# One matmul for the high and low part of the activations, in a two-block fp32 transformer kernel

## The chip, the cores and the metric

The kernel runs on one core of a Trainium2 chip, in one launch. The metric is the device time in microseconds (us). On the core five engines with queues of their own run at once: TensorE (PE, matmuls, with its weight loads as PEld), VectorE (DVE), ScalarE (ACT), GpSimd (POOL) and SyncE (SP, which here issues the DMAs). They wait for each other through semaphores.

## The reference

Everything is fp32, 256 tokens of width 1024. The first block has two layers, the second one; `@` is an fp32 product. Cut to what matters:

```
# first block, each of 2 layers
z = rms_norm(x, norm1_g) @ w_in          # latents, q/k/v of GLA, S5 input, 3 x 1024 gates
merged = sum over b of sigmoid(gate_b) * (mixer_b(z) @ w_br_b)     # MLA, GLA, S5
x = x + merged @ w_out
x = x + square(relu(rms_norm(x, norm2_g) @ w_ff1)) @ w_ff2         # 1024 -> 4096 -> 1024
# second block, 1 layer
z = rms_norm(x, g_pre_mix) @ w_in                     # q, k, v of 24 heads, GLU input, 2 gates
u = (a + b) * sigmoid(g + b)                          # GLU, 1024 channels
c = silu(layer_norm(depthwise_conv_31_taps(u) + b_dw)) @ w_conv_out + b_conv_out
merged = sigmoid(z_ga) * (dilated_attention(q, k, v) @ w_attn_out) + sigmoid(z_gc) * c
x = x + rms_norm(merged @ w_mix_out)
g, up = split(rms_norm(x) @ w_ffn_in)                 # 2 x 2816
x = x + rms_norm((silu(g) * up) @ w_ffn_out)
```

## The kernel before, in words

**Split operands.** TensorE multiplies fp32r, which keeps fewer bits than fp32. So every operand is taken apart into a high part H (ACT `Copy` into an fp32r tile, L160; L163 with a scale) and a low part L = x - H (DVE, L161; L164 with a scale). A product is H·H + H·L + L·H, three matmuls into one PSUM accumulator.

**The weight stream.** The weights come in units of 128x1024 (a row of eight 128x128 blocks). SP starts the DMA of a unit into `raw` (three buffers), ACT makes `wH` and DVE `wL` (four buffers for both together); a unit is fetched three units ahead of the one in use (`AHEAD = 3`).

**Feature-major units.** `f_unit` (L967) is the commonest use of a unit: 128 output features for 256 tokens. `mm_f` (L166) walks eight steps of the contraction, and in each step puts the 256 tokens through three times:

```
nc.tensor.matmul(ps, H[:, w], aH[:, i, :], start=(i == 0), stop=False)             # L169: weights H, activations H
nc.tensor.matmul(ps, H[:, w], aL[:, i, :], start=False, stop=False)                # L170: weights H, activations L
nc.tensor.matmul(ps, L[:, w], aH[:, i, :], start=False, stop=(i == nk - 1))        # L171: weights L, activations H
```

The result takes half of a PSUM bank: the tile `mm` has 128x512, of which `ps[:, :S]` (S = 256) is written. There are two `mm` tiles. One operation then takes it out (`evac`): an ACT copy, tanh, relu or square, or a DVE multiply. The activations lie in two tiles `hH` and `hL`, [128, 8, 256] each. There are 240 such units: the projections w_in of both blocks (38 in each layer of the first block, 56 in the second), w_ff1 (32 in each layer) and both halves of w_ffn_in (44). `mm_f`, or the same three matmuls written out, also serve the eight units of the conformer's output (`conv_out`, eight steps), the eight tiles of the S5 GLU (`s5_glu_tile`, four steps), the branch projections and the attention output.

**Token-major units.** `mm_t` (L173 to L177) puts 512 weight columns past 128 tokens into the accumulator `acc` (five buffers); w_ff2, w_ffn_out, w_out, w_mix_out and the v projections use it. In the FFN stages the units alternate: one `f_unit` (24 matmuls of 256 columns) and one token-major unit (12 matmuls of 512 columns).

**The order of the work.** The order of units and side work (the mixers' steps, the convolution) is written out by hand as strings of tokens; a scheduler then places each instruction on its engine's queue by priorities (taking a result out of PSUM has a raised one). In each engine the instructions run in the resulting order.

**The convolution of the second block.** `conv_gen` takes 31 taps for eight channel tiles `u`, two tiles at a time: DVE starts a sum (L1282), adds a tap times `u` (L1285, 128x256 each), and adds products that ACT made (L1278, 128x512). Its inputs `u` come out of 16 f-units (`g2th`, `ga`, L1451). `chan_sum` then adds the eight sums (L1305 to L1307) and sums over channels on TensorE (L1310); the layer norm and `conv_out` follow. Beside this run the q and k units of the attention and its scores (L1382, L1383).

Of the kernel before, what the change touches and what calls it, by code (L numbers as in the profile page):

```python
# [17 lines left out]
P = 128  # L18
# [17 lines left out]
# columns of the packed per-partition parameters of one layer of the first block  # L36
# [50 lines left out]
class Plan:  # L87
    """Program order: weight units (with what uses them) and side work."""
# [62 lines left out]
def make(k, tc, ins, out, dbg=None):  # L151
    """Fills k with the helpers; returns the plan."""
# [13 lines left out]
    def mm_f(ps, H, L, aH, aL, nk, off=0, m=P):  # L166
        for i in range(nk):
# [3 lines left out]
            nc.tensor.matmul(ps, L[:, w], aH[:, i, :], start=False, stop=(i == nk - 1))  # L171

# [41 lines left out]
    k.__dict__.update(split=split, mm_f=mm_f, mm_t=mm_t, sm=sm, rsq=rsq, mm_tile=mm_tile,  # L214
# [42 lines left out]
def pair_of(h):  # L257
    return lambda c: (h[0], h[1], c)
# [6 lines left out]
def residual_raw(k, t, accs, scale, g, dst):  # L265
    """x[:, t] += accs (times scale); x times g into dst, transposed."""
# [18 lines left out]
def norm_full(k, t, rsn, ss, gb, dst):  # L285
    """rsn[:, t] = rsqrt(mean(x^2) + eps); the normed x into dst, transposed; gb holds g in every row."""
# [8 lines left out]

def row_tile(k, i, name):
# [5 lines left out]
def post_residual(k, t, accs, gb, eps=EPS * D):  # L302
    """x[:, t] += accs rsqrt(sum(accs^2) + eps) gb; gb holds sqrt(D) g."""
# [40 lines left out]
def new_h(k):  # L344
    hH = k.act.tile([P, 8, S], F32R, tag="hH", name="hH")
    hL = k.act.tile([P, 8, S], F32R, tag="hL", name="hL")
    return hH, hL


# ---------------------------------------------------------------- S5  # L350
def s5_setup(k, l, st):
    """First part of what doesn't depend on the activations. The sequence is cut into 64 chunks of 4 steps:
    inside a chunk the output is a short convolution (k.W), chunk inputs go to the states by st.ET, states to
    the outputs by st.F, and the states at the chunk ends are scanned in a rotating frame (tables st.C, st.Sn,
    decay st.D). Parameters lie as [2 groups x 64 states, pair of groups, re/im, 16]; "s" has re and im
    exchanged."""
# [81 lines left out]
def s5_powers(k, st, name, nk, x, xs, ct, op):  # L438
    """[128, 8, nk, 16]: x times powers of lambda, for the four pairs of a channel tile, re and im."""
# [14 lines left out]
def s5_expand(k, dst, src):  # L454
    """Each half of the states to its own 16 of the 32 channels; the rest of dst stays zero."""
# [5 lines left out]
def s5_tile_prep(k, st, ct):  # L461
    """Matrices of one channel tile."""
# [30 lines left out]
def s5_tables(k, st):  # L493
    """Rotating frame of the scan over the chunks."""
# [101 lines left out]
def s5_run(k, l, st, prep):  # L596
    """prep: make what doesn't depend on the activations on the way."""
# [12 lines left out]
def s5_gelu(k, l, st):  # L610
    """2 * gelu(y), and gelu(y) split."""
# [16 lines left out]
def s5_glu_tile(k, l, st, n, H, L, off):  # L628
    nc = k.nc
    ps = k.mm_tile()  # L630
    k.mm_f(ps[:, :S], H, L, st.gH, st.gL, 4, off)
    th = k.t1("gluth")
    nc.scalar.activation(th, ps[:, :S], AF.Tanh, scale=0.5, bias=st.hb[:, n:n + 1])
# [5 lines left out]
# ---------------------------------------------------------------- GLA  # L639
def gla(k, l, st):  # L640
    """Needs st.gq (scaled), st.gk, st.kg, st.gv, st.sr (2 silu(r)); leaves st.goH, st.goL."""
# [24 lines left out]
    nc.vector.tensor_mul(qt, st.gq, E1)  # L666
# [189 lines left out]
def mla_attn(k, l, st, hf):  # L856
    """Heads 4 hf .. 4 hf + 3; needs st.qn, st.kn (per token tile), st.v; writes st.moH, st.moL."""
# [1084 lines left out]
```

## Time and profile before

| | |
|---|---|
| runs | 1485.37, 1485.79, 1486.06 us; median 1485.79 |
| span of the profiled execution | 1482.4 us |
| PE busy | 1440.2 us, 97% of the span, 10580 matmuls |
| PEld (weight loads, beside PE) | 1299.2 us, 88% |
| DVE busy | 1019.1 us, 69% |
| ACT busy | 840.1 us, 57% |
| DMA | 243.13 MB in, mean 164 GB/s |

The profiled execution's own time is its span, first instruction to last; the runs' times are 3 to 4 us above it. A row of the timeline gives an instruction's start and duration. Matmuls are pipelined, so their durations overlap, and what one of them costs is the distance from one start to the next. A granted clock (PEclk) of 1.00 is TensorE's 2.4 GHz, its upper level.

### The profile page before, as it was taken

The numbers are of one execution on the slowest core, as the hardware profiler recorded it, in microseconds if no ns is written. First come the engines' busy times: TensorE is split into PE (matmuls) and PEld (weight loads), VectorE is DVE, ScalarE is ACT, GpSimd is POOL, SyncE is SP. The second block draws the span as 40 slices with busy tenths as digits, with TensorE's granted clock in tenths as the row PEclk, the third lists the DMA queues.
The fourth block names the chain that finished last, engine by engine and source line by source line (L and its number), as shares of the span: only waits on it lengthen the run. The fifth ranks groups of instructions, "written<-read, shape, count | busy, mean of one in ns | idle before, by whom it ended". The sixth has DMA issues, their size and how long they took to land.

```text
span 1482.4 us, 26521 instructions
## 1 busy us (share of the span) xinstructions
PE 1440.2 (97%) x10580; PEld 1299.2 (88%) x10580; DVE 1019.1 (69%) x1876; ACT 840.1 (57%) x1469; POOL 48.6 (3%) x51
## 2 busy tenths in 40 slices
PE   8999999989999999989999999999999999899998
PEld 6979899778889899788988999989888989799997
DVE  7976777687455668566566555579988856765555
ACT  6855567465744556355546444465576574644443
POOL 1000100000000000012000000000000000000000
PEclk9999999999999999999999999999999999999999
DMA  6622344555455653235446555575544545355553
GB/s 223 207 86 97 108 162 152 163 171 183 160 165 186 209 165 94 81 130 171 155 164 218 189 185 186 188 234 178 179 146 121 167 143 206 126 195 185 185 185 114
DMA packets 71060, 243.13 MB, mean 164 GB/s; under 512 B 7864, under 2 KB 11656, under 8 KB 70936
## 3 DMA queue, kind: packets, MB, share of 16 engines
q1 hardware_dynamic: 70936, 241.43, 49.9%
q8 instruction: 83, 1.36, 0.4%
q14 instruction: 41, 0.34, 0.1%
HBM read 237.17 MB, written 4.23 MB: 163 GB/s over the span
## 4 chain that ended last, share of the span: by engine, by line
PE 72%; DVE 9%; ACT 3%; issue 2%; POOL 2%; DMA 1%; POOLq 0%; DVEq 0%; ACTq 0%; SPq 0%
PE mm L169 13%; PE mm L170 13%; PE mm L171 13%; PE acc L175 7%; PE acc L176 7%; PE acc L177 7%; DVE wL L161 3%; POOL rsq L184 2%; ACT wH L160 2%; DVE cv L1285 1%; PE acc L1409 1%; DMA raw<-in_wst_dram 1%; PE tr L1404 1%; PE acc L1382 1%; PE acc L548 1%
## 5 line engine op out<-in xcount | busy, mean ns | idle before, releaser
L161 DVE TENSOR_TENSOR wL<-raw,wH 128x1024 fp32r<-128x1024 f32 (+1 forms) x410 | 495.9, 1211 | 253.7 <-ACT wH L160 250.7
L160 ACT ACTIVATE wH<-raw 128x1024 fp32r<-128x1024 f32 (+1 forms) x410 | 429.2, 1047 | 379.7 <-PE mm L170 199.1
L169 PE MATMUL mm<-hH,wH 128*128 128x256 f32 x1920 | 553.5, 289 | 7.0 <-ACT gt L1038 3.5
L170 PE MATMUL mm<-hL,wH 128*128 128x256 f32 x1920 | 548.5, 286 | 3.2 <-DVE hL L164 3.2
L171 PE MATMUL mm<-hH,wL 128*128 128x256 f32 x1920 | 547.9, 286 | 0.0
L169 PEld LDWEIGHTS mm<-hH,wH 128*128 128x128 f32 x1920 | 368.5, 192 | 21.0 <-ACT hH L163 5.3
L170 PEld LDWEIGHTS mm<-hL,wH 128*128 128x128 f32 x1920 | 368.9, 192 | 8.8 <-DVE hL L164 4.4
L171 PEld LDWEIGHTS mm<-hH,wL 128*128 128x128 f32 x1920 | 368.9, 192 | 2.4 <-issue 1.9
L175 PE MATMUL acc<-wH,fH 128*128 128x512 f32 x344 | 135.3, 393 | 0.0
L176 PE MATMUL acc<-wL,fH 128*128 128x512 f32 x344 | 134.9, 392 | 0.0
L177 PE MATMUL acc<-wH,fL 128*128 128x512 f32 x344 | 134.1, 390 | 0.0
L1285 DVE SCALAR_TENSOR_TENSOR cv<-u,ppt,cv 128x256 f32<-128x256 f32 x184 | 78.6, 478 | 0.4
L177 PEld LDWEIGHTS acc<-wH,fL 128*128 128x128 f32 x344 | 64.6, 188 | 14.1
L175 PEld LDWEIGHTS acc<-wH,fH 128*128 128x128 f32 x344 | 64.9, 189 | 11.2
L176 PEld LDWEIGHTS acc<-wL,fH 128*128 128x128 f32 x344 | 64.9, 189 | 10.3
L160 ACT ACTIVATE fH<-ffr 128x256 fp32r<-128x256 f32 x64 | 26.6, 416 | 67.6 <-DVE ffr L1191 67.5
L161 DVE TENSOR_TENSOR fL<-ffr,fH 128x256 fp32r<-128x256 f32 x64 | 27.1, 424 | 23.2 <-ACT fH L160 23.2
L175 PE MATMUL acc<-wH,mH 128*128 128x512 f32 x96 | 37.9, 395 | 0.3 <-ACT mH L163 0.3
L176 PE MATMUL acc<-wL,mH 128*128 128x512 f32 x96 | 37.8, 394 | 0.0
L177 PE MATMUL acc<-wH,mL 128*128 128x512 f32 x96 | 37.2, 395 | 0.0
L184 POOL TENSOR_TENSOR rsq<-nm,mhalf 128x1 f32<-128x1 f32 x12 | 7.6, 635 | 841.5 <-DVE nm L223 841.5
L164 DVE SCALAR_TENSOR_TENSOR wL<-raw,ppt,wH 128x512 fp32r<-128x512 f32 x40 | 28.4, 747 | 9.1 <-ACT wH L163 9.1
(433 smaller groups left out, 2155.4 us busy)
## 6 DMA issues: line engine op xcount, KB each, us to landing
raw<-in_wst_dram SPq DMA_DIRECT2D x420, 512.0 KB, 3.4
xd<-x SPq DMA_DIRECT2D x6, 512.0 KB, 2.9
x<-xd SPq DMA_DIRECT2D x6, 512.0 KB, 4.3
bias<-bdram SPq DMA_DIRECT2D x8, 384.0 KB, 4.9
gnorm<-in_rows_dram SPq DMA_DIRECT2D x3, 512.0 KB, 5.1
raw<-in_wst_dram SPq DMA_DIRECT2D x4, 384.0 KB, 4.1
x<-in_x_dram SPq DMA_DIRECT2D x4, 256.0 KB, 3.3
x<-in_x_dram SPq DMA_DIRECT2D x2, 512.0 KB, 5.1
```

Source lines behind the costliest of these rows:

```text
L160: nc.scalar.activation(H, src, AF.Copy)
L161: nc.vector.tensor_sub(L, src, H)
L164: nc.vector.scalar_tensor_tensor(L, src, scale, H.bitcast(F32), op0=OP.mult, op1=OP.subtract)
L169: nc.tensor.matmul(ps, H[:, w], aH[:, i, :], start=(i == 0), stop=False)
L170: nc.tensor.matmul(ps, H[:, w], aL[:, i, :], start=False, stop=False)
L171: nc.tensor.matmul(ps, L[:, w], aH[:, i, :], start=False, stop=(i == nk - 1))
L175: nc.tensor.matmul(ps, aH[:, ki, tt], H[:, cols], start=start, stop=False)
L176: nc.tensor.matmul(ps, aH[:, ki, tt], L[:, cols], start=False, stop=False)
L177: nc.tensor.matmul(ps, aL[:, ki, tt], H[:, cols], start=False, stop=stop)
L184: nc.gpsimd.tensor_tensor(o, m, k.mhalf[:, 0:1].to_broadcast([P, n]), op=OP.pow)
L548: nc.tensor.matmul(ps[:, (4 * c + q) * 64:(4 * c + q + 1) * 64], E[:, c, :], us[:, q, :], start=True, stop=True)
L1285: nc.vector.scalar_tensor_tensor(st.cv[:, ct], u(ct, i), w(ct, i), st.cv[:, ct], op0=OP.mult, op1=OP.add)
```

## The change

A product's first two matmuls of a step become one. The activations now lie in one tile `h`, [128, 8, 2, 256], high and low part of a contraction step side by side. `mm_p` streams these 512 columns past the high weights into both halves of the bank, then the 256 high columns past the low weights into the first half. `fold` adds the halves: ACT copies the second half out of PSUM (with the bias, where there is one), DVE adds the first half to it. What was the evacuating operation then works in place on the copy in SBUF.

```diff
+    def mm_p(ps, H, L, a, nk, off=0, m=P):
+        for i in range(nk):
+            w = slice((off + i) * m, (off + i + 1) * m)
+            ai = a(i)
+            nc.tensor.matmul(ps, H[:, w], ai.rearrange("p b n -> p (b n)"), start=(i == 0), stop=False)
+            nc.tensor.matmul(ps[:, :S], L[:, w], ai[:, 0], start=False, stop=(i == nk - 1))
+
+    def fold(out, ps, bias=None, view=lambda a: a):
+        if bias is None:
+            nc.scalar.activation(out, view(ps[:, S:]), AF.Copy)
+        else:
+            nc.scalar.activation(out, view(ps[:, S:]), AF.Identity, bias=bias)
+        nc.vector.tensor_add(out, view(ps[:, :S]), out)
...
 def new_h(k):
-    hH = k.act.tile([P, 8, S], F32R, tag="hH", name="hH")
-    hL = k.act.tile([P, 8, S], F32R, tag="hL", name="hL")
-    return hH, hL
+    return k.act.tile([P, 8, 2, S], F32R, tag="h", name="h")
...
 def f_unit(k, plan, st, blocks, evac, nk=8):
     def run(H, L):
         ps = k.mm_tile()
-        k.mm_f(ps[:, :S], H, L, st.hH, st.hL, nk)
+        k.mm_p(ps, H, L, lambda i: st.h[:, i], nk)
         with k.tc.high_priority(PRI_E):
             evac(ps)
...
     def ff1(n):
         def evac(ps):
             r = k.t1("ffr")
-            nc.scalar.activation(r, ps[:, :S], AF.Relu)
-            nc.vector.tensor_mul(r, r, r)
+            k.fold(r, ps)
+            nc.vector.scalar_tensor_tensor(r, r, 0.0, r, op0=OP.max, op1=OP.mult)
...
+            g = st.gt[b, n // 2][:, n % 2]
+            k.fold(g, ps)
+            nc.scalar.activation(g, g, AF.Tanh, scale=0.5, bias=k.pp("gateb", l)[:, i:i + 1])
...
     def ffu(i):
         def evac(ps):
             s = sg.pop(i)
-            nc.vector.tensor_tensor(s, ps[:, :S], s, op=OP.mult)
+            u = k.t1("ffup")
+            k.fold(u, ps)
+            nc.vector.tensor_mul(s, u, s)
```

All 240 f-units, the eight of `conv_out` and the eight S5 tiles go over to `mm_p`; branch projections and attention output keep `mm_f`. The factor 0.125 of the queries moves into a multiply that was there (GLA) and into the scalar of the attention's score reduction (second block, with the bias table times 8). The inputs of the S5 GLU and of `conv_out` are split in two halves of 128x512 where it was one of 128x1024. Counted over the program: 2016 matmuls and as many weight loads fewer, with as many columns streamed as before; 138 ACT and 260 DVE operations more, 256 of the latter the adds of `fold` (L188).

PE, a token-major unit of the FFN of the first block ends and a w_ff1 unit begins (`h` holds both parts now, `mm` is the PSUM tile). Before:

```order
L177 MATMUL acc<-wH,fL 128x512
L169 MATMUL mm<-hH,wH 128x256
L170 MATMUL mm<-hL,wH 128x256
L171 MATMUL mm<-hH,wL 128x256
L169 MATMUL mm<-hH,wH 128x256
L170 MATMUL mm<-hL,wH 128x256
L171 MATMUL mm<-hH,wL 128x256
```

And now:

```order
L194 MATMUL acc<-wH,fL 128x512
L179 MATMUL mm<-h,wH 128x512
L180 MATMUL mm<-h,wL 128x256
L179 MATMUL mm<-h,wH 128x512
L180 MATMUL mm<-h,wL 128x256
```

Three matmuls of 256 columns became one of 512 and one of 256, and nothing else moved there.

DVE, in the middle of the convolution (`cv` its sums, `u` its inputs, `wL` low weights). Before:

```order
L161 TENSOR_TENSOR wL<-raw,wH 128x1024
L1285 SCALAR_TENSOR_TENSOR cv<-u_11104,ppt,cv 128x256
L1285 SCALAR_TENSOR_TENSOR cv<-u_11173,ppt,cv 128x256
L1285 SCALAR_TENSOR_TENSOR cv<-u_11104,ppt,cv 128x256
L161 TENSOR_TENSOR wL<-raw,wH 128x1024
L1451 SCALAR_TENSOR_TENSOR u_11242<-g2th,ga 128x256
L1285 SCALAR_TENSOR_TENSOR cv<-u_11173,ppt,cv 128x256
```

And now:

```order
L161 TENSOR_TENSOR wL<-raw,wH 128x1024
L188 TENSOR_TENSOR k<-mm,k 128x256
L1313 SCALAR_TENSOR_TENSOR cv<-u_10162,ppt,cv 128x256
L1313 SCALAR_TENSOR_TENSOR cv<-u_10218,ppt,cv 128x256
L1313 SCALAR_TENSOR_TENSOR cv<-u_10162,ppt,cv 128x256
L1313 SCALAR_TENSOR_TENSOR cv<-u_10218,ppt,cv 128x256
L161 TENSOR_TENSOR wL<-raw,wH 128x1024
L188 TENSOR_TENSOR ga<-mm,ga 128x256
```

The adds (L188) stand mostly right behind a `wL`, ahead of taps. Between the first operation of the convolution and the last add of `chan_sum`, DVE's order holds 46 of these adds that were not there, 54 `wL` for 52, and 20 pairs of score reductions for 18.

PE, around the first matmul of `chan_sum`. Before:

```order
L170 MATMUL mm<-hL,wH 128x256
L171 MATMUL mm<-hH,wL 128x256
L1310 MATMUL tr<-cs_13400,cst 128x256
L1381 MATMUL acc<-k,q 128x128
L1382 MATMUL acc<-k,q 128x256
L169 MATMUL mm<-hH,wH 128x256
```

And now:

```order
L180 MATMUL mm<-h,wL 128x256
L179 MATMUL mm<-h,wH 128x512
L1338 MATMUL tr<-cs_12151,cst 128x256
L180 MATMUL mm<-h,wL 128x256
L179 MATMUL mm<-h,wH 128x512
```

48.0 f-units of the second block stood ahead of it, and 50.2 do now.

## Rows read from the trace of the kernel before

**Rows 1.** The page: span, and busy time of each engine.
```profile
span 1482.4 us, 26521 instructions
PE 1440.2 (97%) x10580; PEld 1299.2 (88%) x10580; DVE 1019.1 (69%) x1876; ACT 840.1 (57%) x1469; POOL 48.6 (3%) x51
```

**Rows 2.** The page: the chain that ended last, shares of the span by line.
```profile
PE mm L169 13%; PE mm L170 13%; PE mm L171 13%; PE acc L175 7%; PE acc L176 7%; PE acc L177 7%; DVE wL L161 3%; POOL rsq L184 2%; ACT wH L160 2%; DVE cv L1285 1%; PE acc L1409 1%; DMA raw<-in_wst_dram 1%; PE tr L1404 1%; PE acc L1382 1%; PE acc L548 1%
```

**Rows 3.** Groups: busy us, mean ns | idle before, releaser.
```profile
L169 PE MATMUL mm<-hH,wH 128*128 128x256 f32 x1920 | 553.5, 289 | 7.0 <-ACT gt L1038 3.5
```

**Rows 4.** Timeline of PE, FFN: start, duration, instruction; 21 starts, then 12.
```profile
849.93 0.28 PE L171 MATMUL mm<-hH,wL 128*128 128x256 f32 x1
...
852.45 0.28 PE L171 MATMUL mm<-hH,wL 128*128 128x256 f32 x1
852.57 0.40 PE L175 MATMUL acc<-wH,fH 128*128 128x512 f32 x1
...
853.27 0.40 PE L175 MATMUL acc<-wH,fH 128*128 128x512 f32 x1
...
854.18 0.39 PE L176 MATMUL acc<-wL,fH 128*128 128x512 f32 x1
...
855.09 0.39 PE L177 MATMUL acc<-wH,fL 128*128 128x512 f32 x1
855.32 0.28 PE L169 MATMUL mm<-hH,wH 128*128 128x256 f32 x1
```

**Rows 5.** Windows: length, then PE, PEld, DVE, ACT, POOL, PEclk, DMA share, GB/s.
```profile
20.00:100.00 80.00, 76.80 (x675) 68.51 (x674) 72.00 (x184) 64.32 (x117) 0.22 (x2) 1.00 0.50 165
800.00:900.00 100.00, 100.00 (x641) 91.23 (x641) 57.43 (x72) 47.92 (x72) 0.00 (x0) 1.00 0.58 189
992.00:1178.00 186.00, 184.81 (x1336) 167.25 (x1336) 171.49 (x369) 117.67 (x210) 0.00 (x0) 1.00 0.53 166
1300.00:1400.00 100.00, 100.00 (x706) 94.11 (x705) 57.00 (x71) 44.46 (x59) 0.00 (x0) 1.00 0.57 187
```

**Rows 6.** Timeline of the three engines, end of a w_ff1 unit.
```profile
863.69 0.28 PE L171 MATMUL mm<-hH,wL 128*128 128x256 f32 x1
...
863.94 1.06 ACT L160 ACTIVATE wH<-raw 128x1024 fp32r<-128x1024 f32 x1 [1.56 <-PE mm L170]
...
864.90 0.36 ACT L1190 ACTIVATE ffr<-mm 128x256 f32<-128x256 f32 x1
...
865.03 1.23 DVE L161 TENSOR_TENSOR wL<-raw,wH 128x1024 fp32r<-128x1024 f32 x1 [1.40 <-ACT wH L160]
...
866.17 0.42 DVE L1191 TENSOR_TENSOR ffr<-ffr 128x256 f32<-128x256 f32 x1
```

**Rows 7.** Groups by form: the evacuating operations, of PSUM and of SBUF.
```profile
L1190 ACT ACTIVATE ffr<-mm 128x256 f32<-128x256 f32 x64 | 23.4, 366 | 0.1
...
L1584 DVE TENSOR_TENSOR ffs<-mm,ffs 128x256 f32<-128x256 f32 x22 | 9.3, 424 | 15.3 <-PE mm L171 14.8 <-ACT ffs L1577 0.5
...
L1577 ACT ACTIVATE ffs<-ffs 128x256 f32<-128x256 f32 x22 | 8.8, 401 | 0.2 <-DVE ffs L1576 0.2
```

**Rows 8.** DVE in the convolution, first and last operation; groups of 992 to 1178.
```profile
L1282 DVE TENSOR_SCALAR cv<-u,ppt x8: 402/406/414, 992.1 to 1075.1; 128x256 f32<-128x256 f32 x8
...
1177.81 0.42 DVE L1307 TENSOR_TENSOR cs<-cs 128x256 f32<-128x256 f32 x1
...
L1310 PE MATMUL tr<-cs,cst x2: 377/377/377, 1181.3 to 1181.5; 128*128 128x256 f32 x2
...
L1385 DVE CUSTOM_DVE_ANT_0 sp<-acc,bias 128x256 f32<-128x256 f32 x18 | 7.5, 419 | 0.0
L1383 DVE CUSTOM_DVE_ANT_0 sp<-acc,bias 128x128 f32<-128x128 f32 x18 | 5.2, 288 | 5.2 <-PE acc L1382 5.2
```

**Rows 9.** The chain that ended last, 1030 to 1045: start, length, what.
```profile
1034.52 1.14 DVE wL L161
...
1037.99 2.05 DVE cv L1285 x6
```

More of the change, by code (lines that the diff above doesn't have):

```diff
@@ L123 @@
 class K:
+    pass
 def bcm(ap, n):
@@ L212, in dump_x @@
                 nc.sync.dma_start(dbg[name][:, t, :], k.xt[t])
-    k.__dict__.update(split=split, mm_f=mm_f, mm_t=mm_t, sm=sm, rsq=rsq, mm_tile=mm_tile,
+    k.__dict__.update(split=split, mm_f=mm_f, mm_p=mm_p, fold=fold, mm_t=mm_t, sm=sm, rsq=rsq, mm_tile=mm_tile,
                       acc_tile=acc_tile, tr_tile=tr_tile, t4=t4, t2=t2, t1=t1, dump=dump, dump_x=dump_x)
@@ L293, in norm_full, with pair4, split4 @@
         transpose_half(k, t, q, xn, None, dst)
+def pair4(k, name):
+    return [k.t4(name, (P, 2, 2, S), F32R) for _ in range(2)]
+def split4(k, pair, src, scale=None):
+    for i, t in enumerate(pair):
+        k.split(t[:, :, 0], t[:, :, 1], src[:, 2 * i:2 * i + 2], scale)
 def row_tile(k, i, name):
@@ L630, in s5_glu_tile @@
     ps = k.mm_tile()
-    k.mm_f(ps[:, :S], H, L, st.gH, st.gL, 4, off)
+    k.mm_p(ps, H, L, lambda i: st.gp[i // 2][:, i % 2], 4, off)
     th = k.t1("gluth")
-    nc.scalar.activation(th, ps[:, :S], AF.Tanh, scale=0.5, bias=st.hb[:, n:n + 1])
+    k.fold(th, ps)
+    nc.scalar.activation(th, th, AF.Tanh, scale=0.5, bias=st.hb[:, n:n + 1])
     o4 = k.t1("o4")
@@ L1003, in run @@
                 st.su = k.t4("su", (P, 4, 4, 64))
-            nc.scalar.activation(st.su[:, n], ps[:, :S].rearrange("p (n s) -> p s n", s=4), AF.Copy)
+            k.fold(st.su[:, n], ps, view=lambda a: a.rearrange("p (n s) -> p s n", s=4))
         return run
@@ L1008, in kg_evac, with gqk_evac @@
         st.kg = k.t1("kg")
-        nc.scalar.activation(st.kg[0:64], ps[0:64, :S], AF.Copy)
-    def gqk_evac(name, n, scale):
+        k.fold(st.kg[0:64], ps[0:64])
+    def gqk_evac(name, n):
         def run(ps):
@@ L1014, in run @@
                 setattr(st, name, k.t2(name, (P, 2, S)))
-            nc.scalar.activation(getattr(st, name)[:, n], ps[:, :S], AF.Copy, scale=scale)
+            k.fold(getattr(st, name)[:, n], ps)
         return run
@@ L1021, in run @@
             L = k.main.tile([P, 1, S], F32R, tag="lat", name=name + "L")
-            k.split(H[:, 0], L[:, 0], ps[:, :S], k.pp(gname, l)[:, n:n + 1])
+            x = k.t1("latx")
+            k.fold(x, ps)
+            k.split(H[:, 0], L[:, 0], x, k.pp(gname, l)[:, n:n + 1])
             getattr(st, name + "H")[n] = H
@@ L1125, in run @@
             ps = k.mm_tile()
-            k.mm_f(ps[0:64, :S], H, L, st.hH, st.hL, 8, m=64)
+            k.mm_p(ps[0:64], H, L, lambda i: st.h[:, i], 8, m=64)
             kg_evac(ps)
@@ L1230, in norm1 @@
             spill_x(k, t)
-        nx.hH, nx.hL = h
+        nx.h = h
         k.dump_x(f"x{l}b")
@@ L1335, in conv_ln @@
     yield
-    st.cH = [k.t4("cH", (P, 4, S), F32R) for _ in range(2)]
-    st.cL = [k.t4("cL", (P, 4, S), F32R) for _ in range(2)]
+    st.cp = [pair4(k, "cp") for _ in range(2)]
     for h, c in enumerate(cv):
@@ L1441, in evac @@
             st.ga = k.t1("ga")
-            nc.scalar.activation(st.ga, ps[:, :S], AF.Identity, bias=k.pp("bglua")[:, i:i + 1])
+            k.fold(st.ga, ps, k.pp("bglua")[:, i:i + 1])
         f_unit(k, plan, st, f_blocks("w_in_2", 0, A0 + i * P, 8), evac)
@@ L1447, in evac @@
             th = k.t1("g2th")
-            nc.scalar.activation(th, ps[:, :S], AF.Tanh, scale=0.5, bias=k.pp("bglug")[:, i:i + 1])
+            k.fold(th, ps)
+            nc.scalar.activation(th, th, AF.Tanh, scale=0.5, bias=k.pp("bglug")[:, i:i + 1])
             u = k.main.tile([P, 30 + S], F32, tag="u", name=f"u{i}")
@@ L1453, in glu_gate, with qk_unit @@
         f_unit(k, plan, st, f_blocks("w_in_2", 0, G0 + i * P, 8), evac)
-    def qk_unit(nm, c0, tl, key, scale):
+    def qk_unit(nm, c0, tl, key):
         def evac(ps):
             d = k.main.tile([P, S], F32, tag="qk", name=nm)
-            o = d
             if nm == "q":
-                o = d.rearrange("p (t c) -> p t c", t=2)[:, :, ::-1]
-            nc.scalar.activation(o, ps[:, :S].rearrange("p (t c) -> p t c", t=2) if nm == "q" else ps[:, :S],
-                                 AF.Copy, scale=scale)
+                tok = lambda a: a.rearrange("p (t c) -> p t c", t=2)
+                k.fold(tok(d)[:, :, ::-1], ps, view=tok)
+            else:
+                k.fold(d, ps)
             (st.q if nm == "q" else st.k)[key] = d
@@ L1469, in evac @@
                 d[n // 2] = k.main.tile([P, 2, S], F32, tag="gt", name="z")
-            nc.scalar.activation(d[n // 2][:, n % 2], ps[:, :S], AF.Tanh, scale=0.5)
+            z = d[n // 2][:, n % 2]
+            k.fold(z, ps)
+            nc.scalar.activation(z, z, AF.Tanh, scale=0.5)
         f_unit(k, plan, st, f_blocks("w_in_2", 0, c0 + n * P, 8), evac)
@@ L1500, in run @@
             ps = k.mm_tile()
-            for i in range(8):
-                w = slice(i * P, (i + 1) * P)
-                cH, cL = st.cH[i // 4][:, i % 4], st.cL[i // 4][:, i % 4]
-                nc.tensor.matmul(ps[:, :S], H[:, w], cH, start=(i == 0), stop=False)
-                nc.tensor.matmul(ps[:, :S], H[:, w], cL, start=False, stop=False)
-                nc.tensor.matmul(ps[:, :S], L[:, w], cH, start=False, stop=(i == 7))
+            k.mm_p(ps, H, L, lambda i: st.cp[i // 4][i % 4 // 2][:, i % 2], 8)
             x = k.t1("cox")
-            nc.scalar.activation(x, ps[:, :S], AF.Identity, bias=k.pp("bconv")[:, n:n + 1])
+            k.fold(x, ps, k.pp("bconv")[:, n:n + 1])
             z = zc[n // 2][:, n % 2]
@@ L1575, in evac @@
             s = k.t1("ffs")
-            nc.vector.tensor_mul(s, ps[:, :S], st.rsB)
+            k.fold(s, ps)
+            nc.vector.tensor_mul(s, s, st.rsB)
             nc.scalar.activation(s, s, AF.Silu)
```

37 lines of the change are left out of this document (17 added, 20 removed).

## Prediction, on record before the changed kernel ran

> **What bounds the kernel now.** I read the page first: of a span of 1482.4 us PE is busy for 97%, DVE for 69%, ACT for 57% [rows 1]. The chain that ended last agrees: the three matmul lines of `mm_f` (L169 to L171) and the three of `mm_t` (L175 to L177) hold 60% of the span between them, no other line more than 3% [rows 2]. So I looked for where PE waits. Before the first matmul of a step it stood idle for 7.0 us in 1920 instructions, half of it for the ACT operation that takes a gate out of PSUM [rows 3]: the hand-over of the two `mm` tiles costs something already, though little.
>
> An average hides stages, so I took windows [rows 5]. In both FFN stages PE is busy for 100.00 of 100 us and DVE for 57: there the price of a matmul is the price of the stage. At 20 to 100 us DVE is busy for 72.00 of 80. In the convolution, 992 to 1178, DVE is busy for 171.49 of 186 us while PE still counts 184.81: both engines are nearly full, and 14.5 us is all that DVE has left. The chain there runs through DVE [rows 9], taps and `wL` in turn. The change takes work from PE everywhere and gives DVE more, so the FFN stages decide the gain and the convolution what is given back.
>
> **What a step costs on PE.** A matmul's cost is the distance of starts, not its duration. From the L171 at 849.93 to the one at 852.45 there are 21 starts of 256 columns: 2.52/21 = 0.120 us. From 852.57 to 855.32 there are 12 of 512 columns: 2.75/12 = 0.2292; the first three are 0.70/3 = 0.2333, the four from 854.18 to 855.09 0.91/4 = 0.2275 [rows 4]. A step of `mm_f` takes 3 x 0.120 = 0.360 us. A step of `mm_p` streams as many columns, 512 + 256: 0.2292 + 0.120 = 0.3492, so 0.0108 less. For 2016 steps that is **-21.8 us**. With 0.2275 it is -25.2, with 0.2333 -13.5. I take the mean, as runs of 512 columns show both. What a pair of alternating lengths costs, no row shows; the start after the twelfth 512 is a 256 in its usual place, so I price it as the sum. Weight loads fall from three to two a step and lie beside the matmuls (PEld is not the fuller of the two in any window [rows 5]); they give nothing of their own.
>
> The clock is granted at 1.00 in these windows, the 2.4 GHz level, before and surely after, since PE stays full [rows 5]. 256 columns at that level are 106.7 ns, 512 are 213.3: what lies over is 13 ns for a short matmul and 16 for a long one. So one start less in a step saves roughly one such overhead, 10.8 ns.
> The Trainium skill, page "TensorE: Matmul & The Clock Gate", section "Wait — 56ns, not 53.3ns?", puts the fixed cost of a warm matmul at about 2.5 ns, by which a step would save only that. The row speaks against it: 13 ns. By the page the term would be some 5 us; as a rival it stands below.
>
> **What the fold adds.** 256 adds on DVE. A 128x256 operation with one operand in PSUM lasts 0.424 us [rows 7]; behind another DVE operation it takes less of the queue, as the `wL` of 1.23 us at 865.03 is followed after 1.14 [rows 6]: 0.34. On ACT some 134 operations take a second pass at 0.40 [rows 7], 54 us on an engine that is busy for 840 of 1482: at no price, covered by PE's matmuls; if that cover fails, a gate comes 0.4 us later. DVE's busy time goes from 1019 to about 1019 + 256 x 0.424 = 1127 us, 76% of the span. Over the program that fits; the question is where.
>
> *FFN stages.* 108 of the 240 units, between which a token-major unit gives 2.75 us of other matmuls. ACT copies at 864.90, 1.21 us after the unit's last matmul started, the DVE operation behind it follows a `wL` at 866.17 [rows 6]. A DVE operation stood in this place before (the square), and one more of 0.34 to 0.42 us every 5.6 us (2.88 + 2.75) fits into an engine that is 57% busy [rows 5]. Nothing lost: the next unit has the other bank. Only at the program's end, where nothing covers it, the last gate-and-up unit is later by an ACT copy and an add: **+1** (0.37 + 0.42).
>
> *The convolution.* From its first operation (992.1) to the end of the last add of the channel sum (1178.2) are 186 us [rows 8]. By the order, DVE gets 46 adds there: 46 x 0.34 to 0.42 = 15.6 to 19.5 us; two more `wL`, 2 x 1.14 = 2.3; and two pairs of score reductions, 2 x (0.42 + 0.29) = 1.4 [rows 8]. That is 19.3 to 23.2 us more for an engine with 14.5 idle. If every gap is filled, DVE needs 171.5 + 19.3 to 23.2 = 191 to 195 us; if none, up to 209. PE arrives at L1310 at 1181.3 now, 189.2 after the start; in the new order 2.2 units of 8 x 0.349 = 2.8 us come before it (+6.1), and 55 of its units' steps gain 8 x 0.0108 each (-4.8): 190.5. So the stage loses between 0 and 209 - 190.5 = 18.5 us. The idle time of DVE is short waits for ACT and PE, which a fuller queue closes in part: I take half filled, **+7** (171.5 + 21 + 7 = 199.5 is the top of it, some of which PE spends on matmuls put before the sum). PE would show it as waits for `wL` or at the channel sum, as they all hang on DVE's queue.
>
> *The crowded start*, 20 to 100 us: about 14 adds, 5 us, into 8 us of idle DVE [rows 5]: 0 to 5, taken as **+2**.
>
> *Back-to-back units.* In the other stages (132 units) f-units follow each other with no token-major unit between. The bank of a unit is wanted by the next but one, which is one unit later: 0.12 + 8 x 0.349 = 2.91 us after the last matmul's start. If copy and add come as in [rows 6], the add ends at 866.17 + 0.42 = 866.59, which is 2.90 after that start. The margin is nothing, where a single ACT operation left over a microsecond (864.90 + 0.36 = 865.26, 1.57 after). No row shows how often DVE is late; below, some units are early by a whole `wL`, and then it costs nothing; above, see the rival. I take **+2**, the nearest row being the 7.0 us of idle time of today [rows 3].
>
> The scale factors move into operations that run anyway, and the halved splits of S5 and `conv_out` add four operations on each of ACT and DVE; the first half is ready sooner than the whole was, so I cost them at nothing.
>
> **The sum**: -21.8 + 1 + 7 + 2 + 2 = -9.8; 1482.4 becomes 1472.6. The runs' median, 1485.79, stands 3.4 above the profiled span, so the forecast is **1476.0 us**. A measurement here tells 0.2%, 3 us, from no change: under 1482.8 is faster, over 1488.8 slower.
>
> **Rivals.**
> 1. *DVE's gaps hold it all.* The adds fall into idle time in the convolution too, and the hand-over costs nothing; the fast spacing holds: 1482.4 - 25.2 + 1 + 3.4 = 1461.6. For it: DVE has 31% idle over the span [rows 1]. Against it: 171.49 of 186 [rows 5]. 0.22.
> 2. *The convolution gives back all it can.* No gap is filled, 18.5 for 7: 1476.0 + 11.5 = 1487.5, no change to be measured. For it: waits of DVE there are for weights that come at PE's pace, so gaps would stay. 0.14.
> 3. *The hand-over sets the pace: slower.* In back-to-back units the add stands behind a `wL` and another DVE operation, and PE, which has no third bank, waits for it at L179. Each time one operation more (0.40 us) is ahead than the margin allows, PE loses 0.40. If that is half of 132 units it is +26 for the +2 and +7 that I took: 1476.0 - 9 + 26 = 1493. It decides from where the loss eats the gain of 20.8: some 52 units. For it: the margin of 0.01 worked out above. Against it: an add has a raised priority, and the chain shows runs of six taps (2.05 us) [rows 9] that it may be put ahead of. 0.10.
> 4. *A start fewer saves nothing.* In the alternation of 512 and 256 a long matmul costs two short ones, 2 x 0.120 us, for instance since its successor starts with less of it hidden. The gain is 0 and the losses stand: 1482.4 + 12 + 3.4 = 1497.8. Against it: 0.2292 in runs of 512 [rows 4]; for it, no row has the alternation. 0.04.
> By the rule of the Trainium skill's page "TensorE: Matmul & The Clock Gate" named above it would be nearly this case, 5 us better: an estimate of 1492.8.
>
> That the change doesn't do what it says is left out: the order has 512-column rows in place of pairs of 256.
>
> **How the numbers follow.** The forecast has 0.50, with a range of its own from 1468 (full spacing, small losses) to 1483 (-13.5 for -21.8). Faster: the forecast's 0.50 less a little at its top, and the first rival: 0.70. Same: 0.16, the second rival and that top. Slower: 0.14, the last two. The range leaves out those two and little else: from the first rival, **1461, to 1489**.
>
> **What would show it.** Right: in the FFN windows L179 to L180 is 0.229 and L180 to L179 0.120; an FFN unit pair takes 24 x 0.120 - 8 x 0.349 = 0.09 us less; DVE busy near 1127, ACT near 890; PE's idle time in the convolution has `wL` or the channel sum behind it, and L1338 starts later than its matmuls would put it. Wrong: a spacing of 0.24 after a 512; PE's waits before L179 being for the add L188 and summing to more than 5 us; the convolution's stretch staying under 191 us or passing 209; ACT, or a DMA, as the releaser of most of PE's idle time.

## The result, and the profile after

The changed kernel takes 1536.66 us (median; 1531.33 to 1538.54) against 1485.58 before: a ratio of 1.0335, 95% interval 1.0309 to 1.0361. It is slower by 51 us. The forecast was 1476, the range ended at 1489.

The page of the changed kernel: span, busy time, and the engines' shares of the chain that ended last:

```profile
span 1534.7 us, 22804 instructions
PE 1457.2 (95%) x8564; PEld 1195.8 (78%) x8564; DVE 1104.4 (72%) x2136; ACT 881.2 (57%) x1607; POOL 44.9 (3%) x51
...
PE 76%; DVE 12%; ACT 7%; issue 2%; DMA 2%; POOL 1%; SPq 0%; POOLq 0%; DVEq 0%; ACTq 0%
```

Beside [rows 1], PE has 2016 matmuls fewer and yet 17.0 us more of busy time (1457.2 for 1440.2); outside it, it stands for 77.5 us where it stood for 42.2. DVE and ACT hold 19% of the chain between them. So the loss is in two parts of PE's own time: stops, and matmuls that took longer.

Where? I cut both spans at the first and the last token-major matmul of each FFN. The windows of the changed kernel (columns as in [rows 5]; mixed stage, FFN, mixed, FFN, mixed, FFN):

```profile
0.00:341.54 341.54, 309.85 (x2106) 253.55 (x2107) 253.30 (x596) 213.99 (x426) 20.71 (x25) 0.95 0.43 139
341.54:524.71 183.17, 183.17 (x953) 148.96 (x951) 122.24 (x185) 107.69 (x187) 0.56 (x1) 1.00 0.54 178
524.71:826.37 301.66, 286.41 (x2005) 237.31 (x2004) 210.50 (x427) 168.25 (x327) 17.28 (x16) 0.98 0.45 146
826.37:997.37 171.00, 171.00 (x856) 143.40 (x855) 108.80 (x158) 83.53 (x129) 0.56 (x1) 1.00 0.59 189
997.37:1354.60 357.23, 333.07 (x1748) 265.36 (x1746) 292.60 (x602) 218.23 (x392) 4.74 (x6) 0.96 0.50 155
1354.60:1527.75 173.15, 173.07 (x905) 147.03 (x904) 113.98 (x168) 88.82 (x148) 0.55 (x1) 1.00 0.55 174
```

The mixed stages of the kernel before, cut the same way:

```profile
0.00:316.98 316.98, 297.44 (x2450) 265.92 (x2451) 239.33 (x552) 204.14 (x392) 22.95 (x25) 0.99 0.46 149
...
501.04:796.37 295.33, 285.86 (x2345) 257.48 (x2344) 194.77 (x380) 156.97 (x291) 18.59 (x16) 0.98 0.45 147
...
968.91:1300.37 331.46, 325.65 (x2288) 292.93 (x2286) 269.23 (x530) 208.86 (x362) 4.87 (x6) 0.99 0.52 166
```

All three FFN stages are a little shorter (before: 184.1, 172.5 and 175.1 us), by 0.9, 1.5 and 1.9. The mixed stages are longer: by 24.6, 6.3 and 25.8 us. In the first and the third the granted clock is lower too, 0.95 and 0.96 where it was 0.99; in the second it is 0.98 in both.

What PE waited for, by the waits of the whole span (total us, times, longest); the add of `fold` is L188:

```profile
PE mm L179 <- DVE z L188: 9.0, 4, 5.5
...
PE mm L179 <- DVE gt L188: 6.3, 5, 2.4
...
PE mm L179 <- DVE gluth L188: 2.9, 2, 1.5
...
PE mm L179 <- DVE su L188: 2.2, 1, 2.2
PE mm L179 <- DVE ffr L188: 2.0, 2, 1.2
```

With eight smaller ones PE waited 29.3 us for the add, 23 times (28.1 of it before L179). [Rows 3] had 3.5 us for the one ACT operation in its place. The longest wait can be read in the timeline (start, duration, and idle time before). PE, ACT and DVE in order of time:

```profile
1221.55 2.45 DVE L1313 SCALAR_TENSOR_TENSOR cv<-u,ppt,cv 128x256 f32<-128x256 f32 x6
...
1222.00 0.37 ACT L185 ACTIVATE z<-mm 128x256 f32<-128x256 f32 x1
...
1223.92 0.28 DVE L1411 CUSTOM_DVE_ANT_0 sp<-acc,bias 128x128 f32<-128x128 f32 x1
...
1224.45 0.28 PE L180 MATMUL mm<-h,wL 128*128 128x256 f32 x1
...
1225.08 2.45 DVE L1313 SCALAR_TENSOR_TENSOR cv<-u,ppt,cv 128x256 f32<-128x256 f32 x6
...
1227.45 1.21 DVE L161 TENSOR_TENSOR wL<-raw,wH 128x1024 fp32r<-128x1024 f32 x1
1228.59 1.21 DVE L1333 TENSOR_TENSOR cs<-cv 128x1024 f32<-128x1024 f32 x1
1229.73 0.41 DVE L188 TENSOR_TENSOR z<-mm,z 128x256 f32<-128x256 f32 x1
...
1230.19 0.80 PE L179 MATMUL mm<-h,wH 128*128 128x512 f32 x1 [5.46 <-DVE z L188]
1230.79 0.41 PE L180 MATMUL mm<-h,wL 128*128 128x256 f32 x1
1231.00 0.63 PE L179 MATMUL mm<-h,wH 128*128 128x512 f32 x1
```

The bank that PE wants at 1224.73 is that of the unit before last. ACT had copied its second half by 1222.37. Its add stood behind what was left of six taps, a product of the convolution, two score reductions, six more taps, a split and the first add of the channel sum, and ran at 1229.73, 7.4 us after the copy. The granted clock was 1.00 up to 1227 and 0.50 from 1229 to 1234, so it fell during the stop. Behind the stop the 256 at 1230.79 takes 0.21 us to the next start, and the 512 at 1231.00 takes 0.42 (the next matmul starts at 1231.42): that is TensorE's lower level, 1.2 GHz.

The longest stretch at that level, some 20 us from 108 on, is another matter. These windows show PE full and the clock at half, then rising:

```profile
110.00:120.00 10.00, 10.00 (x60) 7.00 (x59) 4.01 (x9) 1.47 (x4) 0.00 (x0) 0.50 0.00 0
120.00:130.00 10.00, 10.00 (x38) 7.35 (x37) 2.73 (x6) 0.25 (x1) 0.00 (x0) 0.55 0.01 2
130.00:140.00 10.00, 10.00 (x114) 8.37 (x114) 5.33 (x12) 5.61 (x17) 1.02 (x1) 0.83 0.15 54
```

Between 85 and 106 us PE had stopped for 1.1, 0.9 and 1.5 us for operations of the mixers (`s5z`, `gla_kend`, `s5w`), and for 0.3 us for an add; from 103.9 on it ran mostly small matmuls of the mixers. Such matmuls come before a fall with no long stop, too: in the second mixed stage PE was busy for 9.67 of the 10 us from 617 and granted 1.00, then busy for all of the 9.5 us from 627.5 and granted 0.50. From 623.7 on it had run 20 matmuls of one column (L792) and then those of GLA (L756, L759). The kernel before falls to 0.50 at the same place, at 601.

The mean granted clock of the whole span is 0.975 for 0.992. With half of the upper level granted for the rest that is 2 x 0.025 x 1534.7 = 77 us at the lower level for 24, and as matmuls take about twice as long there, up to 26 us of the loss. Of the stretches at that level only two, 10 us in all, have a stop for an add as the nearest one (those that ended at 1209.5 and 1230.2). Whether the adds brought on the others, by making the mixers' operations late or by the order, is not shown.

Last, the step itself. A w_ff1 unit with its token-major neighbour in the changed kernel's FFN, first starts only:

```profile
854.28 0.40 PE L192 MATMUL acc<-wH,fH 128*128 128x512 f32 x1
...
857.07 0.39 PE L179 MATMUL mm<-h,wH 128*128 128x512 f32 x1
...
859.88 0.40 PE L192 MATMUL acc<-wH,fH 128*128 128x512 f32 x1
```

Eight steps take 859.88 - 857.07 = 2.81 us for 2.88, the forecast being 2.79. The twelve 512s before them take 857.07 - 854.28 = 2.79, where [rows 4] has 2.75: more than half of the gain is given back by work that the change didn't touch. In the FFN of the second block nothing is given back: there twelve 512s take 2.75 us before and after. In its order two f-units stand before each token-major one, before and after the change, and not one as in the first block.

### The profile page after: what moved, and what is told of

Read it like the earlier page. It is cut to its first block, busy times and chain, and to the rows that moved or that the text cites. A ratio compares the mean times of both kernels' runs of the same rounds, so it can differ in the third digit from the quotient of the medians.

```text
span 1534.7 us, 22804 instructions
## 1 busy us (share of the span) xinstructions
PE 1457.2 (95%) x8564; PEld 1195.8 (78%) x8564; DVE 1104.4 (72%) x2136; ACT 881.2 (57%) x1607; POOL 44.9 (3%) x51
## 4 chain that ended last, share of the span: by engine, by line
PE 76%; DVE 12%; ACT 7%; issue 2%; DMA 2%; POOL 1%; SPq 0%; POOLq 0%; DVEq 0%; ACTq 0%
PE mm L179 25%; PE mm L180 13%; PE acc L192 8%; PE acc L194 8%; PE acc L193 8%; DVE wL L161 3%; ACT wH L160 2%; DVE cv L1313 2%; PE mm L169 1%; POOL rsq L201 1%; PE mm L170 1%; PE mm L171 1%; DMA raw<-in_wst_dram 1%; PE acc L1437 1%; PE acc L573 1%
## 5 line engine op out<-in xcount | busy, mean ns | idle before, releaser
L179 PE MATMUL mm<-h,wH 128*128 128x512 f32 x1920 | 704.6, 406 | 32.9 <-DVE z L188 9.0
L180 PE MATMUL mm<-h,wL 128*128 128x256 f32 x1920 | 547.7, 286 | 0.0
L179 PEld LDWEIGHTS mm<-h,wH 128*128 128x128 f32 x1920 | 363.8, 190 | 132.2 <-DVE h L164 11.9
L180 PEld LDWEIGHTS mm<-h,wL 128*128 128x128 f32 x1920 | 365.9, 191 | 8.7 <-issue 3.9
L188 DVE TENSOR_TENSOR ffr<-mm,ffr 128x256 f32<-128x256 f32 x64 | 26.8, 418 | 11.1 <-ACT ffr L185 11.1
L1067 ACT ACTIVATE gt<-gt,ppt 128x256 f32<-128x256 f32 x48 | 24.2, 503 | 17.9 <-DVE gt L188 17.9
L192 PE MATMUL acc<-wH,rH 128*128 128x512 f32 x80 | 32.6, 416 | 0.9 <-ACT wH L163 0.9
L163 ACT ACTIVATE wH<-raw,ppt 128x512 fp32r<-128x512 f32 x40 | 26.8, 714 | 10.5 <-DMA raw<-in_wst_dram 3.5
```

Of the source, the lines that this page charges most:

```text
L163: nc.scalar.activation(H, src, AF.Copy, scale=scale)
L179: nc.tensor.matmul(ps, H[:, w], ai.rearrange("p b n -> p (b n)"), start=(i == 0), stop=False)
L180: nc.tensor.matmul(ps[:, :S], L[:, w], ai[:, 0], start=False, stop=(i == nk - 1))
L188: nc.vector.tensor_add(out, view(ps[:, :S]), out)
L192: nc.tensor.matmul(ps, aH[:, ki, tt], H[:, cols], start=start, stop=False)
```

## Experiments

Stages are cut as above, from one profiled execution each. Such an execution can lie 5 us from its kernel's median (e1's took 1494.78, e13's 1490.84). Stages that an edit doesn't touch mostly agree within 1 us, but not all: e5's second mixed stage is 1.8 us over that of before, e12's 2.9 over that of e7, e11's first 3.2 over that of e10. So a difference of a stage under some 3 us tells nothing. "Three banks" means three `mm` buffers and four `acc`. Each ratio is to runs of the kernel before that were timed beside the kernel (medians 1483.8 to 1485.9).

| kernel | median us | ratio to before (95%) | mixed 1 | mixed 2 | mixed 3 |
|---|---|---|---|---|---|
| before | 1485.58 | | 317.0 | 295.3 | 331.5 |
| the change | 1536.66 | 1.0335 (1.0309-1.0361) | 341.5 | 301.7 | 357.2 |
| e1, no add | 1489.66 | 1.0024 (1.0009-1.0040) | 328.5 | 298.9 | 329.7 |
| e2, fold without merge | 1529.96 | 1.0293 (1.0268-1.0318) | 332.7 | 305.5 | 349.4 |
| e3, ACT copies the bank | 1515.51 | 1.0192 (1.0173-1.0211) | 327.2 | 297.7 | 350.5 |
| e4, add on GpSimd | 1550.19 | 1.0447 (1.0424-1.0471) | 342.6 | 307.6 | 352.8 |
| e5, FFN stages only | 1487.40 | 1.0005 (0.9992-1.0019) | 317.6 | 297.1 | 332.8 |
| e6, priority 30 | 1535.59 | 1.0333 (1.0296-1.0371) | 346.8 | 301.2 | 353.1 |
| e7, three banks | 1498.42 | 1.0098 (1.0066-1.0130) | 329.2 | 290.8 | 343.4 |
| e8, five taps fewer | 1518.55 | 1.0229 (1.0208-1.0250) | 341.4 | 302.6 | 338.5 |
| e9, before, three banks | 1486.04 | 1.0002 (0.9984-1.0020) | 319.6 | 297.1 | 331.3 |
| e10, e5 with three banks | 1484.13 | 0.9984 (0.9969-1.0000) | 317.9 | 297.8 | 334.6 |
| e11, e10 and mixed 2 | 1484.29 | 0.9992 (0.9977-1.0007) | 321.1 | 299.0 | 335.3 |
| e12, e7 and e8 | 1485.05 | 0.9998 (0.9984-1.0012) | 327.9 | 293.7 | 330.4 |
| e13, second pass, no merge, no add | 1495.77 | 1.0071 (1.0049-1.0092) | 326.5 | 292.6 | 331.0 |
| e14, merge only | 1486.52 | 1.0010 (0.9994-1.0025) | 329.2 | 295.7 | 327.0 |
| e15, before, halved S5 split | 1486.95 | 1.0009 (0.9992-1.0025) | 316.3 | 295.3 | 331.2 |
| e16, before, second pass | 1495.42 | 1.0059 (1.0023-1.0096) | 324.9 | 295.9 | 331.6 |

My theory after the result: the add holds the bank while it stands in DVE's queue, so PE stops and its clock falls. The first rival: it is the adds' load on DVE, wherever they stand. Others: the merge itself is at fault, or the order of instructions.

**e1, the add left out.**

```diff
-            nc.scalar.activation(out, view(ps[:, S:]), AF.Copy)
+            nc.scalar.activation(out, view(ps[:, :S]), AF.Copy)
...
-        nc.vector.tensor_add(out, view(ps[:, :S]), out)
```

> The fold is an ACT copy of the bank's first half alone: the DVE add is gone, and with it the product of the high weights with the low activations (its columns are still streamed, nobody reads them). If the loss comes from the adds (as the holders of the bank, or as load on DVE), the time falls from 1536.7 to 1470-1480 us: before's 1485.6 less 2016 x 0.008 = 16 us, plus a little for the second pass on ACT; the granted clock returns to 0.99 and PE's waits before L179 fall under 10 us. If the loss comes from the new order of the instructions or from the ACT passes, it stays over 1515 us.

47 us come back: the adds are the larger part of the loss. But 1489.66 is no gain on before, so what the merge should give is lost elsewhere: 11.5 us of it in the first mixed stage, by an execution 5 us over the median. The clock is 0.985, not 0.99.

**e2, the fold without the merge.**

```diff
-            nc.tensor.matmul(ps, H[:, w], ai.rearrange("p b n -> p (b n)"), start=(i == 0), stop=False)
-            nc.tensor.matmul(ps[:, :S], L[:, w], ai[:, 0], start=False, stop=(i == nk - 1))
+            nc.tensor.matmul(ps[:, S:], H[:, w], ai[:, 1], start=(i == 0), stop=(i == nk - 1))
+        for i in range(nk):
...
+            nc.tensor.matmul(ps[:, :S], H[:, w], ai[:, 0], start=(i == 0), stop=False)
+            nc.tensor.matmul(ps[:, :S], L[:, w], ai[:, 0], start=False, stop=(i == nk - 1))
```

> The fold stays, the merged matmul goes: three matmuls of 256 columns a step again, the low activations into the second half of the bank. If a merged step saves the 8 ns that the trace shows (0.3514 for 0.3594), the time rises from 1536.7 by up to 16 us, to 1545-1553 us, less what the longer unit (2.88 for 2.81 us) takes off the stops. If the merge saves nothing, it stays at 1537 or falls.

A miss: with three short matmuls it is 6.7 us faster, not slower. Beside the fold a shorter unit earns nothing, and PE is idle for 66.0 us where it was 77.5. That fits the theory, that PE meets the next bank sooner and waits there, but the scheduler's order differs too, so the 6.7 us are not shown to come from it. The edit also moves a unit's eight low products ahead of its others; in the second FFN ACT's copy still starts 1.21 us after the start of the unit's last matmul, as in the change. What is shown: the fold and what comes with it, without the merge, costs 44 us.

**e3, the bank freed by ACT.**

```diff
+        b = k.main.tile([P, 512], F32, tag="bank", name="bank")[0:ps.shape[0]]
+        nc.scalar.activation(b, ps, AF.Copy)
...
+            nc.vector.tensor_add(out, view(b[:, :S]), view(b[:, S:]))
```

> ACT copies the whole bank (512 columns) to SBUF, and the DVE add reads SBUF: as many adds on DVE as in the changed kernel, but the bank is free when ACT is done. Two t2 buffers and one t4 buffer make room. If the loss is the hand-over of the bank behind DVE's queue, the time falls to 1475-1492 us, the granted clock to 0.985-0.992 and the waits before L179 under 12 us. If it is the load on DVE (late low weights, late convolution), it stays at 1520-1540 us.

Between the two: 21 us come back, 26 stay over e1. The first and second mixed stage are at e1's level, with as many adds on DVE as in the change, which points to the hold there. The third isn't (350.5 for 329.7): in its waits the low weights and the channel sum appear, which no bank has to do with. These two come to 5.1 us; the stage's clock is 0.96 as well. The edit has side effects, too: ACT's copies take 0.58 us for 0.37, PE still waits for them, and there are fewer buffers. So the 26 us are not the adds' load alone.

```profile
PE mm L179 <- ACT bank L184: 7.2, 9, 1.7
PE mm L179 <- DVE h L164: 7.1, 8, 1.2
...
PE mm L180 <- DVE wL L161: 3.0, 1, 3.0
...
PE tr L1341 <- DVE cs L1335: 2.1, 1, 2.1
```

So both theories have a place.

**e4, the add on GpSimd** (as e3, with `nc.gpsimd.tensor_add`).

> As the run in which ACT copies the whole bank, but the add is made by GpSimd out of SBUF: the bank is freed by ACT and DVE has none of the 256 adds. If what was left there (1515.5 against 1489.7 without adds) is the adds' load on DVE, the time falls to 1488-1500 us, provided that GpSimd's add of 256 columns takes under 1.5 us; the convolution's stage returns from 350 to about 332 us. If it is the copies on ACT or the tightened buffers, it stays at 1510-1520.

Worse. By the profile, whose spans are rough on GpSimd, most groups of adds keep the proviso and two small ones don't (`su` 1.80 us, `gq` 1.79). The largest group takes three times DVE's 0.42:

```profile
L186 POOL TENSOR_TENSOR ffr<-bank 128x256 f32<-128x256 f32 x64 | 81.4, 1273 | 378.9 <-ACT bank L184 378.8
```

The first FFN, 182 to 184 us in every other version, is 191.8, and in the mixed stages what follows an add comes later. The 16 adds with a bias stayed on DVE, so it wasn't freed of all 256. The run says nothing on DVE's load.

**e5, the merge and the fold in the FFN stages only.**

> The merged matmul and the fold in the 108 units of the FFN stages alone; everything else as before. Both theories: the FFN stages gain what the traces show for them (0.8 + 1.5 + 1.9 us), the mixed stages stay: 1479-1483 us. If the FFN units contribute to the loss, over 1488 us.

The FFN stages are at 183.4, 171.1 and 173.2, the gain the change has there, 4 us in sum. The total, 1487.40, shows none of it: the mixed stages took 0.6, 1.8 and 1.3 us more. A gain of 0.3% is lost in that, and neither forecast is met.

**e6, the priority of the evacuation** (`PRI_E = 30` for 1).

> The changed kernel with the priority of taking a result out of PSUM raised from 1 to 30, so that the adds come ahead of other DVE work in the order. If the bank is held because the add stands behind taps and splits, the time falls by 5 to 25 us, to 1512-1531, and the waits before L179 for adds from 29 us to under 15. If the order has little to do with it, 1535-1540; if splits of weights that now come later cost as much, over 1540.

No change in the total. The adds' waits fall from 29.3 to 21.3 us only, and the first mixed stage is longer by 5. The adds did come a little sooner: counted over both traces, an add starts 0.83 us after the end of its copy on the average, for 0.93, and 16 of the 256 start over 2 us late, for 24. But one still starts 8.2 us late. So a raised priority did not take the long blocks out of the way, and the run is a weak test of the theory.

**e7, three banks.**

```diff
-    k.ps_acc = pool("ps_acc", 5, space=PS)
-    k.ps_mm = pool("ps_mm", 2, space=PS)
+    k.ps_acc = pool("ps_acc", 4, space=PS)
+    k.ps_mm = pool("ps_mm", 3, space=PS)
```

> The changed kernel with three banks for these results and four instead of five for the others. If the hand-over is what stops PE, a third bank gives an add one unit (2.8 us) more: most of the 21 us that the copy of the whole bank gave, 1512-1522 us. If the bank is not it, 1533-1540; more if the fifth accumulator is missed.

38 of the 51 us come back (35 by the ratios), more than expected, and the clock with them (0.987). The waits for the add are 11.4 us in all, 5 times:

```profile
PE mm L179 <- DVE z L188: 6.8, 2, 5.5
...
PE mm L179 <- DVE gt L188: 3.0, 2, 2.1
...
PE mm L179 <- DVE latx L188: 1.6, 1, 1.6
```

So 18 us of waits for adds are gone, and the time at the lower level falls from 77 to 39 us, worth up to 19. One wait of 5.5 us stays. Over the kernel before there remain 12 us in the first mixed stage and 12 in the third.

**e9, the control: before with three banks.**

> Control: the kernel before with three banks for these results and four for the others, as in the run of the changed kernel that fell to 1498.4. If the third bank mends the hand-over that the change made late, the kernel before, whose one ACT operation frees the bank early, gains little: 1478-1487 us. If a third bank is worth some 30 us to any version, 1450-1465.

Nothing (1.0002). The third bank is worth 38 us to the change and none to the kernel before: the hand-over is what it mends. How the part that goes with the clock hangs on it is not shown.

**e8, five taps of the convolution left out** (`if i in (5, 9, 13, 17, 21): continue`), **and e12, the same with three banks.**

> The changed kernel without 5 of the 31 taps of the convolution (left out: 40 operations of 0.40 us on DVE, 16 us, as much as the 46 adds in that stage cost). If DVE's load sets the pace there, the last mixed stage falls from 357 by 12 to 20 us and the whole to 1517-1526 us, the other stages stay. If only the hand-over does, under 6 us.

> The changed kernel with three and four banks and without 5 of the 31 taps (left out). If the hand-over and the load of the adds on DVE in the convolution are two causes that add up, 1498.4 - 12 to 18 = 1480-1487 us; if the third bank took care of both, 1492-1499.

e8 gives 18 us, nearly all in the third mixed stage (338.5). With three banks the taps still give 13 (1498.42 to 1485.05). By the ratios it is 16 and 15. So the load on DVE in the convolution is a cause of its own, and the two add up within a few us. The kernel before without these taps was not run, so it isn't known whether that stage would gain as much there.

**e10 and e11, the change where it is cheapest, with three banks.**

> The merge in the 108 units of the FFN stages alone, with three and four banks. The FFN stages gain 2, 3 and 2 us as in the changed kernel with three banks, the mixed stages are the control's: the control less 4 to 7 us.

> As the run before, and the merge also in the mixed stage of the second layer (where the changed kernel with three banks took 291 us for before's 295). If stages are independent, 4 to 5 us under the run before, if the control's own second mixed stage isn't as fast already; in that case the same or slower.

e10 is 1.9 us under its control e9, not 4 to 7. In the profiled executions its FFN stages are shorter than e9's by 8.5 us in sum (182.2, 169.6 and 171.8 for 184.3, 172.7 and 175.1), and its third mixed stage is longer by 3.3. e10 is under the kernel before by 0.16%, with an interval that ends at 1.0000; e11 adds nothing. No version here beats before by an amount that can be told.

**e13 to e16, the first mixed stage.** Where the hold of the bank is mended or the add is gone (e1, e3, e7, e12), it stays at 327 to 329 us for 317. e13 takes e1 and gives it three matmuls of 256 columns, all into the first half; e14 takes e1 and lets tanh and splits read the bank, as before; e15 and e16 edit the kernel before.

> No merge and no add: three matmuls of 256 columns into the first half, an ACT copy out of PSUM, and the second pass on ACT as in the changed kernel (all products are there). The first mixed stage takes 317 us before and 327 to 329 in every version with the merge. If the second pass on ACT (or the order that it brings) costs that, it is 325-330 here too and the whole 1493-1503 us; if the merge costs it, 317-320 and 1484-1490.

> The merge alone in the mixed stages: no add, and no second pass where it was tanh or a split (taken out of the first half; the product with the low activations is left out, though streamed). If the merge saves 5 ns a step and nothing else hangs on it, 1475-1480 us, with 315-318 in the first mixed stage; if the merge itself costs the first stage its 10 us, 325 there and 1484-1492.

> The kernel before, with one side effect of the change alone: the input of the S5 GLU split in two halves of 128x512 instead of one of 128x1024 (two operations more a layer on each of ACT and DVE). If this small edit, or the order that the scheduler makes of it, costs the first mixed stage its 10 us, that stage takes 325-329 us; if not, 317-320 and the whole 1484-1488.

> The kernel before, with the second ACT pass alone (copy out of PSUM, then tanh or split in place) in the mixed stages: 90 ACT operations more, no merge, no add, no new tiles for the activations. If the pass (or its order) costs the first stage its 10 us, 325-329 us there and 1492-1500 in all; if not, 317-320 and 1484-1490.

The halved split costs nothing. The second pass on ACT costs 8 to 10 us in that stage with nothing else changed (e16: 324.9; e13: 326.5), and 10 us in all, with an interval of 3 to 14 (e16). But the merge without that pass is there too (e14: 329.2), and both together are no longer than either (e1: 328.5). So the second pass is enough to cost it, and something in the merged version is as well. In e14 the granted clock of that stage is 0.96, for 0.98 in e16 and 0.99 before, which can be up to 10 of its 12 us. In each case the scheduler makes another order of the whole stage; whether the order or the operations do it stays open, and wasn't tried further.

One pair of runs differs in the merge alone: beside the second pass and without adds it gains 6 us (e1 against e13; the two intervals don't meet). Without that pass in the mixed stages there is no gain to be seen (e14 against before).

## Why the prediction was wrong

The failed steps, by what they are worth:

- **"Back-to-back units ... I take +2".** This is the step that failed. Its own working had a margin of 0.01 us and a mean of one DVE operation in the way; I then took the smallest row, today's 7.0 us of idle time, which is the price of an ACT operation on an engine that is half idle. The measured price is 38 us (e7 against the change, with e9 as control), of which 18 are waits for adds and up to 19 go with the clock. The prediction's own sign of being wrong, waits before L179 for the add of over 5 us, was met with 28.1. The waits are not 66 of 0.40 us, as the third rival had them: 23 carry 29.3 us, one of them 5.5, where the add met whole blocks of taps and a split. I had such a block in [rows 9] (2.05 us) and used it as an argument for the add being put ahead of it. And I left the clock out of the price of a stop: it was granted at 0.50 after that wait, and the whole span has 77 us at that level for 24. For most of that time the trace shows other stops ahead of it, or small matmuls and none.
- **"The convolution, +7".** From its first operation to the end of the channel sum's last add it took 208.7 us (1022.6 to 1231.3, with 189.82 of DVE busy): the top of my bound, 209, with 18.9 us of gaps kept. So none of the gaps were filled, which was the second rival. Part of that is the hand-over again; by e8 and e12 the load itself is 13 to 18 us. Its sign, waits for `wL` or at the channel sum, did not come: PE's longest wait there is for the add of a `z`.
- **"On ACT ... at no price".** The second pass costs 10 us (e16), in the first mixed stage. I argued it from an engine that is busy for 57% of the span, where I should have asked the stage. There ACT and DVE work in turns for the mixers, and a pass more may delay the next one's turn; that is argued and not shown.
- **"-21.8" for the merge.** A mis-sized term. By the starts in the second FFN a step takes 351 ns for 359, so 8 ns and not 10.8, and a token-major unit behind it takes 36 ns more, so that a pair gains 27 of the 86 ns that I forecast. For 2016 steps at 8 ns that is 16 us, less 64 x 0.036 = 2 in the first block's FFN stages: about 14. The runs show less still: 6 us (e1 against e13), or nothing (e14).

The runs can be put in a chain: the second pass with the small edits around it (e13, +10), then the merge (e1, -6), then the adds (the change, +47), together the 51 us measured. Of the adds' 47 the third bank takes back 38; with it, leaving out as much work on DVE as the adds brought to the convolution gives 13, which together is 4 more than there was. But the prices hold in this order only: without the second pass the merge gains nothing (e14), and each run has an order of its own. So it is a fair account and not more.

The third rival had mechanism and sign, with 26 us; I gave it 0.10, since I took priority and spare DVE time as a protection that a fixed order of the queue does not give. The second rival came true beside it. I had set both against the forecast as alternatives, though one engine's queue is at the bottom of both, and they came together: the range had no room for the sum.

What the prediction had right: that the FFN stages gain and the mixed stages decide; the sum of the two spacings within 2 ns (351.1 for 349.2), though not the two themselves (0.235 and 0.116 for 0.229 and 0.120); the bound of the convolution. DVE's busy time rose by 85 us where 108 were forecast (1104.4 for 1127).

By the fixed cost that the Trainium skill's page "TensorE: Matmul & The Clock Gate", section "Wait — 56ns, not 53.3ns?", states, 2.5 ns a matmul, a step would gain 2.5; the trace has 8, and less with what is given back. The measurement decides: the overhead of a short matmul here is 13 ns (120 for 106.7).

## What to carry to other kernels

Where a second engine is put between a matmul and the release of its PSUM bank, price the longest block that can stand ahead of it in that engine's order, not the mean of its spare time; one bank more, with the kernel before as a control, tells whether that is the cost. Two losses that go through the same queue aren't alternatives, and both belong into the range. A gain on the engine that bounds a stage is worth only what the next work in the same stage doesn't give back: measure it as a pair of units, in their alternation. And follow each stretch at a lower clock back to the stops and the small matmuls before it, before putting it down to the wait that is in mind.

## What the runs showed of the hardware

- In the second FFN a 256-column matmul after a 512 starts its successor after 0.116 us and not 0.120, and the 512 ahead of it takes 0.235. In the first block's FFN stages the runs of twelve 512s between such units take 2.79 us for 2.75; in the second block's, behind two units, they take 2.75 as before.
- After one stop of 5.46 us the following matmuls ran at the lower level (0.42 us to the next start for a 512, 0.21 for a 256, for 0.235 and 0.116), and a stretch at a granted clock of 0.50 with PE fully busy lasted some 20 us (from 108 on). At 627 in the change, and at 601 before, the clock fell to 0.50 with PE busy for 97% of the 10 us ahead, after 20 matmuls of one column and some of 128 columns with weights 64 wide.
- GpSimd's add of 128x256 out of SBUF took 0.74 to 1.80 us by group, by its rough spans; DVE's with one operand in PSUM took 0.42.
